# A hybrid diffusion step on one core: the products of the second four gates, spread over the four units of a long convolution

## Chip, core and metric

The kernel runs on one core of a Trainium2 chip. The metric is the device time of one execution in microseconds (us). The core's engines work from queues of their own: TensorE (PE in the rows, its weight loads PEld), VectorE (DVE), ScalarE (ACT), GpSimd (POOL) and SyncE (SP, which issues the transfers). Each engine takes its instructions strictly in order, and waits where an operand is not ready.

## What is computed

One inference step of a backbone with four layers: a Hyena long convolution, latent attention, RWKV-7, and a Hyena long convolution again. Only the two Hyena layers, the first and the last, are touched. Cut to what matters, the reference computes in each of them, for 1024 latent tokens and 128 context tokens and a width of 1024:

```python
u = h @ w_in                                   # 1024 x 4096
u3, z = u[..., :3 * HY_WIDTH], u[..., 3 * HY_WIDTH:]
prev, nxt = _neighbours(u3)
u3 = prev * conv_w[0] + u3 * conv_w[1] + nxt * conv_w[2] + conv_b
x0, x1, v = jnp.split(u3, 3, axis=-1)
v = v * x1
vf = jnp.fft.rfft(v, n=2 * L, axis=1)
kf = jnp.fft.rfft(filt, axis=0)
y = jnp.fft.irfft(vf * kf[None], n=2 * L, axis=1)[:, :L] + v * skip
return (y * x0 * jax.nn.silu(z)) @ w_out
```

## The kernel before

**Numbers.** All products are float32 in three passes: each operand is split in a high part (ACT, line 267) and a low part (POOL or DVE, line 268), and `mm3` (lines 260 to 264) issues high times high, high times low, low times high. One three-pass product of a 128x128 weight block with 384 tokens is three rows `ps_mm<-hh,wh`, `<-hl,wh`, `<-hh,wl`. They are called *product rows* here.

**Dense products.** `dense_jobs` (line 477) goes through a list of jobs. A job is one block of 128 columns of `w_in`; it has three *steps*, one for each group of 384 tokens, and a step is 24 product rows. After a step the job's own `evac` takes the result out of PSUM. A job for `v`, `x1` or `x0` ends with the convolution of three neighbours: two DVE rows on line 1006. Then `v * x1` is one DVE row on line 1023. A *gate* is the pair of jobs for `x0` and `z` of one block (`jobs_gate`, line 1031): eight gates in a layer. From the fifth on they are "late" (line 1034): ACT applies SiLU to each step's result (line 1047), DVE multiplies it by `x0` at once (line 1040, four pieces), and SP writes it out (line 1049).

**The long convolution** runs in four *units* of 256 channels (`conv_long`, line 1078), one after the other. A unit has three *stages*. *Forward*: transposes of `v` on PE (line 1073), ACT copies them to `xt` (line 1075), and some 42 DVE rows (lines 642 to 711) make eight residues. *Residue*: nine residues go through PE (`ps_fw`), DVE (line 1108), POOL (lines 1110 and 1111), ACT and POOL splits, and PE again (`ps_iv`): 210 PE rows in a unit. *Inverse*: some 47 DVE rows (lines 713 to 800) make `yc`, which SP writes to DRAM (line 1148). `xt` and `yc` use one buffer, so the next unit's copies to `xt` wait until that write has landed. What follows the fourth unit is `boundary` (line 497), the product with `w_out`; its first tile needs `yc` of all four units.

**What sets the order.** `GATES` (line 220) says how many gates go beside each part of the layer: the first number is for the making of the filters ahead of the units, the other four are for the units. `hyena` (lines 1150 to 1158) makes one list of jobs from it, in which the `v` and `x1` jobs of a unit stand beside the unit before, and `steps[q + 1]` is how many steps unit `q` is given. `weave` (line 165) hands out the turns of the unit, of the dense steps and of the modulation parts (`mod_part`, lines 290 to 330; eight DVE rows on line 302 and eight POOL rows on line 305 for a part) in proportion. This is only the order in which the program is written. A scheduler, which follows a timeline of its own, then sets the order on each engine, and moves rows far from where they were written.

Of the kernel before, what the change touches and what calls it, by code (L numbers as in the profile page):

```python
# [216 lines left out]
NM = 52  # L217
NE = 12
MZ = 12
GATES = (4, 0, 0, 0, 4)  # L220


class Prog:
# [745 lines left out]
    def hyena(self, i, j, lead, rest):  # L969
# [46 lines left out]
        def jobs_vx(q):  # L1016
            def dst(b):
                if b == 0:
                    vxs[q] = pool.tile([P, 2, W], F32, tag="vx", name="vx")
                return vxs[q][:, b]  # L1020

            def times(b):
                return lambda x1: v.tensor_tensor(vxs[q][:, b], vxs[q][:, b], x1, ALU.mult)

            r = []
            for b in range(2):
                r.append(conv3(16 + 2 * q + b, lambda b=b: dst(b), lambda d: None))
                r.append(conv3(8 + 2 * q + b, row, times(b)))
            return r

        def jobs_gate(b):

            s = {}
            late = b >= GATES[0]

# [115 lines left out]
        b = 0  # L1151
        for q, n in enumerate(GATES):
            new = jobs_vx(q) if q < NU else []
# [1185 lines left out]
```

## Time and profile before

| | us |
|---|---|
| median of three runs | 4577.58 |
| lowest and highest of the three | 4571.88, 4580.07 |
| the profiled execution's own time | 4590.18 |
| its span, first to last instruction | 4588.4 |
| the four units of the first layer in it, first copy to `xt` to last write of `yc` | 457.3 |
| the four units of the last layer in it | 415.4 |

The page and the queries of the trace are of the profiled execution. TensorE's records are pipelined, so the distance between two starts is what a row costs, not its duration. A stretch's granted clock is 1.00 at 2.4 GHz and 0.5 at 1.2 GHz; values between are means over the stretch.

### The profile page before, as it was taken

How to read it: one execution, taken by the hardware profiler on the slowest of the kernel's cores; microseconds unless marked ns; L12 is line 12 of the kernel's file. 1: busy time of each engine (PE TensorE's matmuls, PEld its weight loads, DVE VectorE, ACT ScalarE, POOL GpSimd, SP SyncE). 2: the span in 40 equal slices, each digit the busy share in tenths (PEclk: the TensorE clock that was granted, in tenths of full speed). 3: DMA queues.
4: the chain of work that ended last, by engine and by line, in shares of the span. 5: the costliest groups of instructions: out<-in, count | busy, mean ns of one | idle time of the engine just before them, and what ended most of it. 6: DMA issues, size and time to landing. Idle time of an engine off the chain costs nothing. (4 is left out here: it accounts for less than half of the span.)

```text
span 4588.4 us, 83899 instructions
## 1 busy us (share of the span) xinstructions
PE 4061.0 (89%) x30888; PEld 3510.6 (77%) x30888; DVE 3504.3 (76%) x6147; ACT 2392.5 (52%) x5468; POOL 2360.3 (51%) x1902
## 2 busy tenths in 40 slices
PE   7988988889999999879979786999999889988988
PEld 4888888678777776658867575878888678878986
DVE  7777888655998999687587997677767668967877
ACT  5554433455666666453455553666666456543331
POOL 3655766253677877455555564333333233466550
PEclk8999999999999999989988797999999899999999
DMA  5755555643000000326635464222322424665455
GB/s 169 239 181 176 164 156 157 191 149 99 19 22 21 18 28 30 121 91 203 188 108 198 145 222 136 59 79 84 83 75 68 142 93 120 214 205 153 141 155 179
DMA packets 490982, 583.04 MB, mean 127 GB/s; under 512 B 59818, under 2 KB 378332, under 8 KB 489932
## 3 DMA queue, kind: packets, MB, share of 16 engines
q1 hardware_dynamic: 489068, 576.70, 40.7%
q8 instruction: 244, 4.00, 0.4%
q14 instruction: 166, 1.36, 0.1%
q10 hardware_dynamic: 1504, 0.98, 0.1%
HBM read 413.74 MB, written 161.37 MB: 125 GB/s over the span
## 5 line engine op out<-in xcount | busy, mean ns | idle before, releaser
L262 PE MATMUL ps_mm<-hh,wh 128*128 128x384 f32 x1728 | 597.0, 347 | 47.4 <-ACT hh L267 24.0
L263 PE MATMUL ps_mm<-hl,wh 128*128 128x384 f32 x1728 | 595.6, 345 | 2.8 <-DVE hl L268 1.8
L264 PE MATMUL ps_mm<-hh,wl 128*128 128x384 f32 x1728 | 594.5, 344 | 2.7 <-POOL wl L268 2.7
L1499 POOL TENSOR_TENSOR sm<-sm,pf 128x512 f32<-128x512 f32 x288 | 443.4, 1540 | 121.8 <-ACT pf L1492 48.8
L268 POOL TENSOR_TENSOR wl<-wraw,wh 128x512 fp32r<-128x512 f32 x212 | 331.5, 1581 | 187.4 <-ACT wh L267 175.3
L262 PEld LDWEIGHTS ps_mm<-hh,wh 128*128 128x128 f32 x1728 | 335.9, 195 | 55.5 <-ACT hh L267 25.1
L1497 DVE TENSOR_TENSOR wl<-pf,wh 128x512 fp32r<-128x512 f32 x288 | 352.8, 1235 | 6.6 <-ACT wh L1493 5.8
L263 PEld LDWEIGHTS ps_mm<-hl,wh 128*128 128x128 f32 x1728 | 336.2, 195 | 7.5 <-DVE hl L268 4.4
L264 PEld LDWEIGHTS ps_mm<-hh,wl 128*128 128x128 f32 x1728 | 336.0, 194 | 6.4 <-POOL wl L268 3.8
L305 POOL TENSOR_TENSOR macc<-macc,mprod 128x512 f32<-128x512 f32 x140 | 211.8, 1513 | 178.0 <-ACT mprod L304 155.4
L263 PE MATMUL ps_mm<-mx,wh 128*128 128x384 f32 x680 | 253.6, 373 | 37.9 <-DVE mx L1669 36.9
L262 PE MATMUL ps_mm<-mx,wh 128*128 128x384 f32 x680 | 255.9, 378 | 19.9 <-ACT mx L1668 6.1
L262 PE MATMUL ps_mm<-woh,hh 128*128 128x512 f32 x576 | 233.8, 407 | 37.0 <-ACT hh L267 34.6
L2144 POOL TENSOR_TENSOR tot<-SV,wcs 64x128 f32<-64x128 f32 x288 | 115.6, 405 | 267.9 <-DVE SV L2172 245.2
L264 PE MATMUL ps_mm<-mx,wl 128*128 128x384 f32 x680 | 247.0, 364 | 3.1 <-POOL wl L268 3.1
L1492 ACT ACTIVATE pf<-ps_st 128x512 f32<-128x512 f32 x288 | 172.3, 598 | 144.9 <-POOL sm L1499 53.3
L264 PE MATMUL ps_mm<-woh,hl 128*128 128x512 f32 x576 | 234.1, 406 | 3.7 <-DVE hl L268 3.7
L302 DVE SCALAR_TENSOR_TENSOR macc<-modw,cond,macc 128x512 f32<-128x512 f32 x140 | 156.5, 1118 | 103.3 <-DMA modw<-mod_w 102.4
L1437 DVE TENSOR_REDUCE mx<-ps_pj 128x1 f32<-128x512 f32 (+2 forms) x400 | 220.4, 575 | 17.2 <-PE ps_pj L1436 16.4
L263 PE MATMUL ps_mm<-wol,hh 128*128 128x512 f32 x576 | 231.8, 402 | 0.0
L304 ACT ACTIVATE mprod<-modw,cond 128x512 f32<-128x512 f32 x140 | 101.3, 723 | 205.5 <-POOL macc L305 108.6
L1493 ACT ACTIVATE wh<-ps_st 128x512 fp32r<-128x512 f32 x336 | 194.3, 578 | 0.0
(560 smaller groups left out, 13149.2 us busy)
## 6 DMA issues: line engine op xcount, KB each, us to landing
cst<-cst SPq DMA_DIRECT2D x175, 384.0 KB
modw<-mod_w SPq DMA_DIRECT2D x160, 256.0 KB
wraw<-hy_w_in SPq DMA_DIRECT2D x128, 256.0 KB
kd<-kt SPq DMA_DIRECT2D x72, 384.0 KB
kt<-kd SPq DMA_DIRECT2D x72, 384.0 KB
cst<-cst SPq DMA_DIRECT2D x41, 512.0 KB
ctd<-ct SPq DMA_DIRECT2D x24, 768.0 KB
bkd<-bk SPq DMA_DIRECT2D x24, 768.0 KB
```

The costliest lines, as they stand in the source:

```text
L262: mm(ps, lh, rh, start=start, stop=False)
L263: mm(ps, lh, rl, start=False, stop=False)
L264: mm(ps, ll, rh, start=False, stop=stop)
L268: (lo_eng or self.nc.gpsimd).tensor_tensor(lo, src, hi, ALU.subtract)
L302: nc.vector.scalar_tensor_tensor(acc[0], w, s, acc[0], op0=ALU.mult, op1=ALU.add)
L305: nc.gpsimd.tensor_tensor(acc[1], acc[1], wp, ALU.add)
L1437: nc.vector.tensor_reduce(mx[:, t, j:j + 1], ps, AX.X, ALU.max)
L1492: nc.scalar.activation(pf, s, AF.Exp, scale=scale)
L1493: nc.scalar.activation(ph, s, AF.Exp, scale=scale)
L1497: nc.vector.tensor_tensor(pl, pf, ph, ALU.subtract)
L1499: nc.gpsimd.tensor_tensor(sm, sm, pf, ALU.add)
L2144: g_.tensor_tensor(tot[h], SV[e][h, jsl], wc[h].unsqueeze(2).broadcast_to([64, 2, 64]), M)
```

## The change

One number table changes; nothing that is computed does.

```diff
-GATES = (4, 0, 0, 0, 4)
+GATES = (4, 1, 1, 1, 1)
```

`steps` goes from (36, 12, 12, 12, 24) to (36, 18, 18, 18, 6): gates 4, 5, 6 and 7 are written beside units 0, 1, 2 and 3 in place of all beside unit 3. Which gates are "late" stays, since `GATES[0]` does. No instruction is added or removed on PE, DVE, ACT or POOL, and the same transfers are issued. What the scheduler makes of it on three places follows.

DVE at the end of the first unit's inverse, first layer. Lines 796, 799 and 754 are the inverse, 1040 a piece of a gate, 302 a modulation step, 651 the first row of the next unit. Before:

```order
L792 SCALAR_TENSOR_TENSOR st<-st 128x256
L302 SCALAR_TENSOR_TENSOR macc_4531<-modw,cond,macc_4531 128x512
L1023 TENSOR_TENSOR vx<-vx,xx 128x1153
L992 MEMSET up 128x1 x3
L796 TENSOR_TENSOR st<-st 128x256
L799 TENSOR_TENSOR st<-st 128x256
L993 MEMSET xx 128x1
L754 SCALAR_TENSOR_TENSOR yc<-st,yc 128x2x128 x2
```

And now:

```order
L1040 TENSOR_TENSOR xx<-xx 128x384
L302 SCALAR_TENSOR_TENSOR macc_4676<-modw,cond,macc_4676 128x512
L796 TENSOR_TENSOR st<-st 128x256
L799 TENSOR_TENSOR st<-st 128x256
L302 SCALAR_TENSOR_TENSOR macc_4676<-modw,cond,macc_4676 128x512
L754 SCALAR_TENSOR_TENSOR yc<-st,yc 128x2x128 x2
L796 TENSOR_TENSOR st<-st 128x256
L799 TENSOR_TENSOR st<-st 128x256
L993 MEMSET vx 128x1 x2
L302 SCALAR_TENSOR_TENSOR macc_4676<-modw,cond,macc_4676 128x512
L1040 TENSOR_TENSOR xx<-xx 128x256
L1040 TENSOR_TENSOR xx<-xx 128x128
```

Right behind this piece stand the last two rows on line 754: the pieces of gate 4 have moved in front of the end of the first unit's inverse.

DVE at the end of the last unit's inverse, last layer. Line 1006 is the convolution for gate 7, 1191 and 268 `hl` are the boundary's. Before:

```order
L785 SCALAR_TENSOR_TENSOR st<-st 128x256
L787 TENSOR_TENSOR st<-su 128x256
L1006 SCALAR_TENSOR_TENSOR xx<-up,cw,xx 128x1153
L788 TENSOR_TENSOR st<-su 128x256
L1191 TENSOR_TENSOR wh<-wh,wl 128x768
L1006 SCALAR_TENSOR_TENSOR xx<-up,cw,xx 128x1153
L791 SCALAR_TENSOR_TENSOR st<-st 128x256
L792 SCALAR_TENSOR_TENSOR st<-st 128x256
L268 TENSOR_TENSOR hl<-wh,hh 128x6x128
L1040 TENSOR_TENSOR xx<-xx 128x384
L796 TENSOR_TENSOR st<-st 128x256
```

And now:

```order
L785 SCALAR_TENSOR_TENSOR st<-st 128x256
L787 TENSOR_TENSOR st<-su 128x256
L788 TENSOR_TENSOR st<-su 128x256
L791 SCALAR_TENSOR_TENSOR st<-st 128x256
L792 SCALAR_TENSOR_TENSOR st<-st 128x256
L796 TENSOR_TENSOR st<-st 128x256
L799 TENSOR_TENSOR st<-st 128x256
L754 SCALAR_TENSOR_TENSOR yc<-st,yc 128x2x128 x2
```

The gate's and the boundary's rows have left the last inverse.

PE at the last inverse product of the last unit, last layer (`ps_iv`); `ps_mm<-woh,hh` is the boundary's first row. Before:

```order
L262 MATMUL ps_iv<-cst,zh 128x256
L263 MATMUL ps_iv<-cst,zh 128x256
L264 MATMUL ps_iv<-cst,zl 128x256
L263 MATMUL ps_mm<-hl,wh 128x384
L264 MATMUL ps_mm<-hh,wl 128x384
```

And now:

```order
L262 MATMUL ps_iv<-cst,zh 128x256
L263 MATMUL ps_iv<-cst,zh 128x256
L264 MATMUL ps_iv<-cst,zl 128x256
L262 MATMUL ps_mm<-woh,hh 128x512
L263 MATMUL ps_mm<-wol,hh 128x512
```

Before, 143 product rows stood between the last inverse product and the boundary there (116 in the first layer); now none do, in either layer.

How many product rows stand on PE between the first `ps_fw` row of residue 1 and the unit's last `ps_iv` row, counted in the two orders:

| unit | first layer, before | now | last layer, before | now |
|---|---|---|---|---|
| 0 | 120 | 192 | 116 | 141 |
| 1 | 160 | 172 | 126 | 144 |
| 2 | 106 | 144 | 146 | 192 |
| 3 | 141 | 32 | 124 | 60 |

## Rows read from the trace of the kernel before

**Rows 1.** Page, part 1: busy us, share and instructions of each engine.

```profile
PE 4061.0 (89%) x30888; PEld 3510.6 (77%) x30888; DVE 3504.3 (76%) x6147; ACT 2392.5 (52%) x5468; POOL 2360.3 (51%) x1902
```

**Rows 2.** Windows, units of either layer: stretch, length; PE, PEld, DVE, ACT, POOL busy; clock; DMA.

```profile
354.80:812.10 457.30, 399.53 (x2431) 386.44 (x2429) 373.93 (x618) 180.91 (x355) 293.68 (x221) 0.94 0.53 162
...
4053.00:4468.40 415.40, 374.33 (x2310) 362.64 (x2308) 317.90 (x565) 156.51 (x317) 247.66 (x191) 0.95 0.51 156
```

**Rows 3.** Windows, first layer: residue, inverse stage of units 0 to 3; forward of 3.

```profile
372.80:427.50 54.70, 49.86 (x330) 47.34 (x330) 36.90 (x55) 21.65 (x43) 41.46 (x36) 0.97 0.64 203
427.50:469.00 41.50, 29.09 (x165) 28.70 (x164) 38.30 (x68) 13.44 (x26) 16.22 (x14) 0.84 0.37 116
...
490.80:553.40 62.60, 56.37 (x360) 54.40 (x361) 48.07 (x56) 26.25 (x51) 60.07 (x45) 0.95 0.64 202
553.40:597.00 43.60, 39.03 (x224) 38.39 (x221) 40.91 (x70) 17.05 (x33) 19.88 (x14) 0.96 0.40 121
...
617.30:663.90 46.60, 44.45 (x319) 43.56 (x320) 32.59 (x42) 17.92 (x35) 44.50 (x37) 1.00 0.75 233
663.90:705.00 41.10, 33.12 (x183) 32.33 (x181) 37.95 (x65) 12.87 (x25) 17.62 (x13) 0.91 0.43 128
705.00:722.20 17.20, 15.14 (x76) 14.82 (x76) 15.15 (x37) 6.40 (x13) 8.28 (x4) 0.81 0.32 90
722.20:777.90 55.70, 50.12 (x336) 48.80 (x337) 37.42 (x47) 21.28 (x40) 44.46 (x39) 0.97 0.64 196
777.90:812.10 34.20, 28.17 (x150) 26.37 (x148) 33.59 (x66) 12.34 (x23) 14.81 (x8) 0.95 0.51 143
```

**Rows 4.** Windows, last layer: residue, inverse stage of units 0 to 3.

```profile
4071.00:4129.50 58.50, 50.56 (x320) 46.82 (x319) 40.23 (x59) 21.57 (x43) 42.32 (x37) 0.94 0.63 194
4129.50:4173.20 43.70, 31.84 (x181) 31.16 (x179) 38.88 (x65) 14.85 (x30) 18.84 (x15) 0.84 0.37 107
...
4191.10:4238.70 47.60, 47.55 (x318) 47.21 (x319) 28.21 (x42) 19.98 (x39) 40.95 (x37) 0.94 0.72 221
4238.70:4271.90 33.20, 32.55 (x194) 32.23 (x193) 30.86 (x62) 11.24 (x27) 10.58 (x9) 1.00 0.34 103
...
4290.40:4341.40 51.00, 49.52 (x335) 48.29 (x336) 34.32 (x49) 20.99 (x42) 42.27 (x36) 0.97 0.68 210
4341.40:4368.30 26.90, 26.90 (x159) 26.90 (x158) 24.88 (x53) 7.64 (x16) 8.67 (x7) 1.00 0.41 128
...
4383.60:4435.40 51.80, 48.23 (x314) 47.62 (x315) 30.15 (x40) 16.54 (x33) 39.11 (x35) 0.93 0.58 182
4435.40:4468.40 33.00, 29.40 (x161) 27.63 (x159) 29.27 (x55) 11.62 (x23) 14.38 (x6) 1.00 0.42 123
```

**Rows 5.** Timeline of PE, two runs of rows: start, duration, row, idle before.

```profile
446.67 0.33 PE L262 MATMUL ps_mm<-hh,wh 128*128 128x384 f32 x1
...
448.58 0.34 PE L264 MATMUL ps_mm<-hh,wl 128*128 128x384 f32 x1
...
4434.09 0.28 PE L262 MATMUL ps_iv<-cst,zh 128*128 128x256 f32 x1
...
4435.05 0.28 PE L264 MATMUL ps_iv<-cst,zl 128*128 128x256 f32 x1
```

**Rows 6.** Groups of DVE by line: count, busy us, mean ns, idle before.

```profile
L1023 DVE TENSOR_TENSOR vx<-vx,xx 128x1153 f32<-128x1153 f32 x16 | 24.4, 1526 | 0.1
...
L302 DVE SCALAR_TENSOR_TENSOR macc<-modw,cond,macc 128x512 f32<-128x512 f32 x140 | 156.5, 1118 | 103.3 <-DMA modw<-mod_w 102.4
```

**Rows 7.** Groups of DVE in the last inverse of the last layer.

```profile
L1006 DVE SCALAR_TENSOR_TENSOR xx<-up,cw,xx 128x1153 f32<-128x1153 f32 x2 | 3.9, 1936 | 0.0
...
L1040 DVE TENSOR_TENSOR xx<-xx 128x384 f32<-128x384 f32 (+1 forms) x3 | 1.5, 507 | 0.0
...
L1191 DVE TENSOR_TENSOR wh<-wh,wl 128x768 f32<-128x768 f32 x1 | 1.0, 959 | 3.1 <-PE ps_mm L264 3.1
```

**Rows 8.** Timeline of PE: the wait ahead of the second unit's transposes, first layer.

```profile
461.33 1.97 PE L1073 MATMUL ps_tp<-ident,vx 128*128 128x128 f32 x8 [12.41 <-DVE up L992]
```

## The prediction

> **What bounds the kernel now.** I read part 1 of the page first. PE is busy for 89% of the span [rows 1], the most of all engines, but that share is a mean over stages with different limits. So I then read the windows over the two places that the change touches. The four units take 457.3 us in the first layer and 415.4 us in the last, 872.7 of 4588.4 us [rows 2]; all else keeps its instructions and, but for small shifts, its order. Last I read the same windows by stage [rows 3, 4], and what ends the waits there.
>
> The reader is to see three different limits. In a *residue* stage PE and POOL are both near full: POOL 44.50 of 46.60 us in unit 2 of the first layer, 60.07 of 62.60 in unit 1, PE 49.52 of 51.00 in unit 2 of the last [rows 3, 4]. In an *inverse* stage of the first layer DVE is full: 38.30 of 41.50, 40.91 of 43.60, 37.95 of 41.10, 33.59 of 34.20 [rows 3]. In the last layer PE has hardly a gap from unit 1's residue stage to unit 2's end: 47.55 of 47.60 and 26.90 of 26.90 [rows 4]. The units follow each other through one buffer, so a unit is a chain of its three stages, and dense products only fill PE beside it. Products that sit between a unit's own rows in PE's queue lengthen it as soon as PE has no gap left; gate rows in DVE's queue lengthen an inverse.
>
> PE waits long in one kind of place: 12.41 us ahead of the second unit's transposes in the first layer [rows 8]. The products that the change brings into unit 0 fill it. That alone gains nothing, since DVE is busy all through that stage; it puts PE ahead by as much.
>
> **The change part by part.** No engine gains or loses rows, so all is a matter of where they stand. Prices: a product row costs 0.173 us (446.67 to 448.58 is eleven of them), a row of `ps_fw` or `ps_iv` 0.12 (4434.09 to 4435.05 is eight) [rows 5]. So a unit's 210 own rows are 25 us of PE, and a residue stage with n products needs n x 0.173 + 25 us of it. On DVE a convolution is two rows, 3.9 us together [rows 7], a row of `v * x1` is 1.53 us, a modulation row 1.12 [rows 6], a gate's piece 0.51, so 2.0 for four [rows 7].
>
> *Residue stages of units 0 to 2.* With the counts in the table of the two orders: first layer, unit 0 needs 58.2 us in place of 45.8 and took 54.70; some of its idle time is filled, so I put it at 60, +5.5. Unit 1 needs 54.8 and took 62.60 with POOL full: no change. Unit 2 needs 49.9 in place of 43.3 and took 46.60: 53, +6.5. Last layer: unit 0 needs 49.4 and took 58.50 on waits of other kinds, +1; unit 1 needs 49.9 in place of 46.8 and took 47.60, +3; unit 2 needs 58.2 in place of 50.3 and took 51.00, +8. Sum **+24**. From below it is 0, if waits that the rows show give way for all of it (PE idle 4.8, 6.2, 2.2, 7.9, 0.1 and 1.5 us in these six stages); from above 24 and those waits again, some +40. I take 24, near to the rows without a gap.
>
> *Forward and inverse stages of units 0 to 2.* Read from DVE's order. First layer: four pieces come into unit 0's inverse and one modulation row leaves it (+1); seven modulation rows leave unit 1's, the pieces and a `v * x1` row come (-4.5); unit 2's forward stage gets five modulation rows and loses a convolution (+2), its inverse gets a convolution, `v * x1` and one modulation row (+6.5). Last layer: pieces into unit 0's inverse (+2); a convolution into unit 1's forward stage (+4), one out of its inverse against the pieces (-2); a convolution and `v * x1` into unit 2's inverse (+5.5). Sum +14.5 if all of it lands. The six inverse stages hold 18 us in which DVE is idle (3.2, 2.7, 3.2, 4.8, 2.3, 2.0 [rows 3, 4]), so from below it is 0. I take **+7**, half, since either end has rows for it.
>
> *The last unit.* First layer: a convolution enters its forward stage and two pieces less run there (+3.5 on 17.20). Its residue stage loses 109 of 141 products: PE needs 30.5 us, and the cover is then POOL, 44.46 busy. I take 48 for 55.70: -8 (from -11 to 0). Its inverse was 34.20 with DVE full. Out of it go a convolution (3.9), the pieces (2.0) and the boundary's row 1191 and its split of the same shape (1.9 for both) [rows 7], together 7.8; with less work of POOL beside it I put it at 24, -10. Last layer: residue stage 51.80 to 44 (POOL 39.11), -8; inverse 33.00 to 21.5, since the same rows go and the wait of 3.1 us for a product [rows 7] with them: -11.5. Sum **-34**, from -45 (stages at POOL's and DVE's bare time) to -18 (residue stages unchanged, since transfers for nine residues come in the same row).
>
> *The end.* Before, 116 and 143 products covered PE during the last inverse; now nothing does. That costs nothing by itself: the boundary's first tile waits for `yc` in either case. SP issues the same transfers; gate writes now stand ahead of the write of `yc` in units 0 to 2, and wait there for pieces that DVE's order has in front of it anyway.
>
> Sum: +24 + 7 - 34 = -3 us against the profiled execution's 4590.18, so 4587. That execution was 12.6 us above the median of the runs, and I carry the difference over to it: 4577.58 - 3 = **4575 us**.
>
> *The clock.* The seventeen stages that have a row here ran at a granted clock of 0.93 or more but four: unit 0's inverse in either layer (0.84), in the first layer that with the wait of rows 8; one other inverse stage (0.91); and the last unit's forward stage in the first layer (0.81) [rows 3, 4]. The last unit's residue stages now hold 30 to 35 us of PE work in 44 to 48, a smaller share than any residue stage has in the rows. The Trainium skill (TensorE: Matmul & The Clock Gate, "What's actually happening") says that half rate is the default state and that activity releases it. By that rule part of these stages would run at half speed, and the sum would come out above the time before; by the rows as they stand it is -3. I make it a rival below.
>
> **Rivals.** *A: the early units hold their pace.* PE's wait of 12.41 us is filled and PE runs ahead by that, so the +24 and +7 shrink to some +5 while -34 stays: about -29, 4549 us. For it: 18 us of DVE and 23 us of PE idle in the stages concerned. Against it: unit 2 of the last layer, where PE has no gap to give.
>
> *B: slower, by the gate's pieces in DVE's queue.* In units 0 to 2 the inverse's last rows now stand behind the gate's pieces, so `yc` cannot end before the gate's last product but one. PE reaches that some 144 products and 18 transposes after the last `ps_iv`, 27 us, and ACT, DVE and the rest of the rows add 2. The inverse stages took 41.50, 43.60, 41.10, 43.70, 33.20 and 26.90 us, of which some 5 are the wait for the write [rows 3, 4]: room of 8 to 10 us in four of them, none in the last two. From the point where PE loses more than that room, every microsecond delays the next unit and all that follows. At 4 us for each of six units it is +24 on the sum: +21, 4599 us. For it: PE waits of 12 us exist. Against it: the change fills the one that is known.
>
> *C: slower, by the clock in the thinned last unit.* At 1.2 GHz a spacing doubles, so the residue stages would need 61 and 71 us of PE in place of 48 and 44, +40; half of each stage there gives +20: +17, 4595 us. Against it: the 55.70 us stage with waits inside stayed at 0.97 [rows 3].
>
> *D: the change does not do what it says.* The scheduler had already moved products ahead: the counts before are far from 12, 12, 12 and 24 steps. Then the time stays within the measurement; my forecast is near to it anyway.
>
> **How the numbers follow.** This kernel's measurement tells 0.2%, 9 us, from no change. My forecast with D: 0.47, own range -15 to +8, of which 0.13 is below -9 and 0.34 within. A: 0.26, from -14 to -45, all faster. B: 0.18, from +6 to +35. C: 0.09, from +9 to +30. Of B 0.01 lies within. So faster 0.39, same 0.35, slower 0.26. With a tenth left out at either end, the range runs from about -32 to +20: 4546 to 4598 us.
>
> **What would show it.** In the profile after, the windows by stage: the residue stages of unit 0 (first layer) at about 60 and unit 2 (last layer) at about 59 us, the last inverses at about 24 and 21.5, the last residue stages at about 48 and 44 with POOL near full. The wait of rows 8 should be gone. The fourth unit should start some 15 to 18 us later in either layer than before, counted from the first copy to `xt`. If it starts no later, A is right; if later by over 25 us, with DVE idle ahead of pieces of a gate (line 1040, released by ACT), B is. Half clock over more than a third of the last residue stages would be C. I would be wrong altogether if the time went into the attention or RWKV layers, whose rows shift a little in the order.

## The result, and the profile after

The changed kernel is slower: 4612.18 us (median of four, 4609.14 to 4621.68) against 4578.82, a ratio of 1.0077 with a 95% interval of 1.0056 to 1.0098. That is +33 us where -3 was forecast, and outside the range of 4546 to 4598. The profiled execution took 4621.68 us, its span 4619.9: 31.5 us more than before. Executions of one kernel lie up to some 30 us apart (before, in one row of runs: 4572.52 to 4601.36), and a trace is of one execution, so sums over two traces that differ by 10 or 20 us decide little; the medians do.

The page after, part 1, and then the windows over the four units of either layer (stretch, length; PE, PEld, DVE, ACT, POOL busy; clock; DMA share, GB/s), answer to [rows 1, 2]:

```profile
PE 4068.9 (88%) x30888; PEld 3513.1 (76%) x30888; DVE 3492.9 (76%) x6147; ACT 2387.2 (52%) x5468; POOL 2351.0 (51%) x1902
```

```profile
354.05:831.20 477.15, 403.58 (x2431) 387.62 (x2429) 370.86 (x615) 179.64 (x355) 284.24 (x221) 0.92 0.51 157
4073.85:4502.55 428.70, 377.91 (x2312) 363.75 (x2310) 320.95 (x566) 154.60 (x318) 248.67 (x191) 0.95 0.50 153
```

The units grew from 457.3 to 477.15 and from 415.4 to 428.70 us, +33.1 together, which is all of it. Rows and busy times of the engines hardly changed, so what changed is how much of the work lies beside other work. The stages of the first layer, as in [rows 3] (units 0 to 2: residue, inverse; unit 2's forward stage ahead of its own; all three of unit 3):

```profile
372.00:430.85 58.85, 58.63 (x398) 58.02 (x398) 33.41 (x57) 24.64 (x50) 43.28 (x37) 1.00 0.65 197
430.85:479.25 48.40, 44.28 (x244) 41.67 (x243) 42.34 (x73) 15.26 (x31) 21.09 (x14) 0.96 0.38 118
...
502.30:570.30 68.00, 55.87 (x363) 54.96 (x362) 48.49 (x62) 27.26 (x54) 51.51 (x43) 0.92 0.61 193
570.30:599.60 29.30, 29.30 (x182) 29.20 (x182) 26.25 (x62) 8.28 (x18) 6.47 (x5) 1.00 0.28 88
599.60:625.95 26.35, 21.18 (x113) 20.45 (x111) 24.40 (x35) 12.95 (x25) 15.57 (x10) 0.94 0.40 120
625.95:687.55 61.60, 52.23 (x350) 51.22 (x350) 38.58 (x58) 23.53 (x49) 46.83 (x39) 0.94 0.59 190
687.55:735.10 47.55, 42.90 (x248) 42.48 (x248) 42.42 (x69) 15.12 (x32) 21.25 (x16) 0.94 0.41 120
735.10:748.45 13.35, 12.44 (x70) 11.48 (x68) 11.27 (x23) 6.86 (x15) 2.98 (x2) 0.96 0.49 151
748.45:804.70 56.25, 38.97 (x232) 36.41 (x232) 41.74 (x58) 17.12 (x30) 39.66 (x36) 0.82 0.58 188
804.70:831.20 26.50, 9.07 (x34) 7.08 (x34) 25.47 (x55) 6.58 (x11) 11.32 (x6) 0.68 0.41 119
```

The same of the last layer, as in [rows 4] (residue, inverse of each unit; unit 2's residue stage from the row on that waited for its operand `sl`, as the 4290.40 of [rows 4] is):

```profile
4091.75:4148.90 57.15, 51.83 (x346) 50.66 (x346) 36.37 (x55) 23.07 (x47) 43.20 (x37) 0.97 0.62 194
4148.90:4197.35 48.45, 42.72 (x244) 40.09 (x242) 42.35 (x73) 15.24 (x31) 21.07 (x14) 1.00 0.39 117
...
4215.85:4274.95 59.10, 52.23 (x349) 51.31 (x349) 35.68 (x54) 22.92 (x48) 42.16 (x37) 0.94 0.64 191
4274.95:4306.20 31.25, 31.25 (x188) 31.08 (x188) 28.02 (x62) 8.97 (x22) 11.10 (x7) 1.00 0.31 100
...
4319.95:4382.35 62.40, 58.81 (x397) 58.12 (x398) 36.67 (x52) 24.62 (x51) 50.10 (x41) 1.00 0.63 197
4382.35:4414.10 31.75, 31.75 (x193) 31.58 (x192) 27.92 (x57) 8.95 (x22) 11.14 (x7) 1.00 0.33 103
...
4429.80:4480.10 50.30, 39.38 (x242) 37.34 (x242) 34.95 (x44) 14.28 (x25) 34.15 (x31) 0.87 0.57 179
4480.10:4502.55 22.45, 7.43 (x18) 5.21 (x18) 21.71 (x48) 5.13 (x9) 5.77 (x4) 0.65 0.32 94
```

Unit by unit, from first copy to first copy: +11, -8, +28, -11 us in the first layer; +3, +10, +11, -12 in the last. Three things are to be seen. Unit 0's inverse grew by 6.9 and 4.8 us, and DVE's busy time in it by 4.0 and 3.5, with the gate's four pieces in it. Unit 1's inverse in the first layer fell by 14.3: it lost the modulation rows, and unit 2 got them. And the last unit's residue stage, which lost three quarters and half of its dense products, stayed as it was: 56.25 for 55.70, 50.30 for 51.80.

### The profile page after: what moved, and what is told of

It is laid out like the page before. It is cut to its first block, busy times and chain, and to the rows that moved or that the text cites. A ratio compares the mean times of both kernels' runs of the same rounds, so it can differ in the third digit from the quotient of the medians.

```text
span 4619.9 us, 83929 instructions
## 1 busy us (share of the span) xinstructions
PE 4068.9 (88%) x30888; PEld 3513.1 (76%) x30888; DVE 3492.9 (76%) x6147; ACT 2387.2 (52%) x5468; POOL 2351.0 (51%) x1902
```

## Which gate costs, and where

Three runs write one gate alone beside an early unit (`GATES` as shown), and one leaves the change as it is but makes gates 4 to 6 in one go after their third step.

```diff
-GATES = (4, 1, 1, 1, 1)
+GATES = (4, 1, 0, 0, 3)   # move_u0; (4, 0, 1, 0, 3) move_u1; (4, 0, 0, 1, 3) move_u2
```

> Gates (4, 1, 0, 0, 3): only one gate is moved, from the last unit to unit 0, in either layer. In the profile after the change unit 0 is longer by 11.1 us in the first layer and 3.0 in the last, and the last unit shorter by 11.1 and 11.6 for three gates. Theory 'each gate costs where it is put': +14 for unit 0, a third of -23 for the last unit, so about +6 us, 4585. Theory 'product rows on PE' (a gate is 144 product rows, the same price in each unit: 55.6 us for three gates, 18.5 each): +11 us, 4590. Theory 'the unit that follows pays': units 1 and 2 change too although they get no gate, and the sum is not that of the profile.

> Gates (4, 0, 1, 0, 3): only one gate is moved, to unit 1. After the change unit 1 is shorter by 7.6 us in the first layer and longer by 10.2 in the last. Theory 'each gate costs where it is put': +2.6 and a third of -23, about -5 us, 4574. Theory 'product rows on PE': +11 us, 4590. Theory 'the unit that follows pays': unit 2 is longer, as it is after the change (+27.5 and +11.4), and the sum is about +10 or more.

> Gates (4, 0, 0, 1, 3): only one gate is moved, to unit 2. After the change unit 2 is longer by 27.5 us in the first layer and by 11.4 in the last. Theory 'each gate costs where it is put': +39 and a third of -23, about +31 us, 4610. Theory 'product rows on PE': +11 us, 4590. Theory 'the unit that follows pays': unit 2 stays near its length before, and the time within 10 us of 4579.

Measured against before: move_u0 1.0004 (0.9986 to 1.0021), move_u1 1.0051 (1.0036 to 1.0065), move_u2 1.0004 (0.9985 to 1.0022). To read them, one has to see where the scheduler put the gates. A gate has three SiLU rows on ACT (line 1047). How many of them start beside units 0 to 3 in each trace:

| kernel | first layer | last layer |
|---|---|---|
| before | 0, 0, 4, 8 | 0, 0, 3, 9 |
| after, nolow_spread, both_spread | 3, 3, 3, 3 | 3, 3, 3, 3 |
| move_u0 | 3, 0, 4, 5 | 3, 0, 3, 6 |
| move_u1 | 0, 3, 2, 7 | 0, 3, 0, 9 |
| move_u2 | 0, 0, 4, 8 | 0, 0, 3, 9 |
| one_last | 0, 0, 9, 3 | 0, 0, 9, 3 |
| one_spread | 3, 3, 6, 0 | 3, 3, 6, 0 |
| nolow_last | 0, 0, 4, 8 | 0, 0, 4, 8 |
| nodve_last | 0, 0, 3, 9 | 0, 0, 3, 8, and one behind |
| nodve_spread | 3, 2, 4, 3 | 3, 2, 3, 4 |
| both_last | 0, 0, 6, 6 | 0, 0, 6, 6 |

Written beside unit 3, gate 4 stood beside unit 2 already in the kernel before, in either layer. So the change takes two gates out of the last unit and not three, and move_u2 is in effect the kernel before: its time says nothing about a gate beside unit 2. move_u1 takes gate 4 from unit 2 to unit 1, and that costs 23 us (16 to 30); where they lie its trace can't tell, since it is of the fastest of the eleven executions (4593.97 us, median 4606.86), with units that take 873.8 us together, near the 872.7 of before. move_u0 takes one gate from the last unit to unit 0 for +2 us (-6 to +10): not the +11 of one price for each gate, while +6 is within. The third expectation, that the unit which follows pays, holds in move_u1 for the first layer (unit 2 at 128.2 us for 108.0) and not for the last (96.1 for 96.5). One thing stands out in move_u0's stages: with one gate gone, its last unit is as short as after the change (93.6 and 91.1 us against 96.1 and 88.5). So the second gate taken out of the last unit brings nothing that these traces show.

```diff
-            late = b >= GATES[0]
+            late = b == 7
```

> The changed kernel, with the gates of units 0 to 2 (4, 5 and 6) made as the first four are: ACT copies each step, and SiLU, the multiplication by x0 and one write follow after the third step. Theory 'gate pieces and gate writes in the queues of DVE and SP hold the unit': their number falls from 4 to 2 rows and from 3 to 1 writes for a gate and none waits for a step in the middle, so half or more of the +33 us goes, 4595 or less. Theories 'product rows on PE' and 'rows of DVE lengthened while POOL works': neither count changes, so the time stays within 8 us of 4612.

whole_spread: 1.0049 (1.0030 to 1.0069), some 13 us of the 35 that the ratio of the change stands for. That is between the two expectations, and its interval overlaps that of the change; by itself it settles nothing.

## Which engine charges for it

Each pair leaves out one engine's rows of gates 4, 5 and 6 in both orders of work. The rows on the other engines stay, but the scheduler makes the order anew for each kernel: the table above tells how near each stays to the one that it is made from. If an engine sets the price, the difference between the two kernels of its pair goes.

PE: one pass in place of three, 288 product rows fewer in either layer.

```diff
-                self.mm3(o, wh[:, k], wl[:, k], self.hh[g][:, k], self.hl[g][:, k], k == 0, k == KC - 1)
+                if len(jobs[n]) > 3 and jobs[n][3]:       # gates 4, 5, 6
+                    self.nc.tensor.matmul(o, wh[:, k], self.hh[g][:, k], start=k == 0, stop=k == KC - 1)
+                else:
+                    self.mm3(o, wh[:, k], wl[:, k], self.hh[g][:, k], self.hl[g][:, k], k == 0, k == KC - 1)
```

> The kernel before (gates 4 to 7 beside the last unit), with the products of gates 4, 5 and 6 made in one pass in place of three: 288 of PE's product rows are left out in either layer, 50 us each at 0.173 us. The control for the next kernel; it says what those rows cost beside the last unit. Theory 'product rows on PE': up to 100 us less in all, since the last unit and the end behind it hold most of them. Theories of DVE, POOL or queues: less than half of that.

> The changed kernel with the same 288 rows of gates 4, 5 and 6 left out in either layer. Against the control: theory 'product rows on PE': the change's +33 us falls to a third, +12 us or less. Theory 'rows of DVE lengthened while POOL works' and theory 'queues' (all rows of DVE, POOL and SP are still there): it stays at +25 to +40 us.

one_last 1.0003 (0.9991 to 1.0016), one_spread 1.0053 (1.0033 to 1.0073). A hundred microseconds of PE's rows were left out and the kernel before did not become faster. The difference is still 0.50%, 23 us (12 to 34), between the 12 or less of one theory and the 25 to 40 of the others. The pair is not a clean one: in one_last all three gates stand beside unit 2, in one_spread two do and none beside unit 3, and unit 0's inverse takes 57.9 us there in place of 48.4. Fewer products and another order are mixed in both, so that dense products have no price of their own is not shown.

POOL: the low parts of these gates' weights are not made (24 rows).

```diff
-        self.load_split(wh, wl, src)
+        if not low:                                       # gates 4, 5, 6
+            for ks in (slice(0, 4), slice(4, KC)):
+                raw = self.wp.tile([P, 4, P], F32, tag="wraw", name="wraw")
+                nc.sync.dma_start(raw, src.rearrange("(k p) n -> p k n", p=P)[:, ks])
+                nc.scalar.copy(wh[:, ks], raw)
+            return wh, wh
```

> The kernel before, with the low part of the weights of gates 4, 5 and 6 not made (the high part stands in for it in the products, so PE's rows are all there): 12 POOL rows of 1.55 us are left out in either layer. The control for the next kernel. Theory 'rows of DVE lengthened while POOL works': a POOL row costs DVE about 1.1 us where DVE is full, so up to 26 us less. Theory 'product rows on PE': no change beyond 8 us.

> The changed kernel with the same 24 POOL rows left out. Against its control: theory 'rows of DVE lengthened while POOL works': the rows now stand beside stages that DVE fills, so the change's +33 us falls by some 15 to 25 us. Theory 'product rows on PE' and theory 'queues': it stays within 8 us of +33.

nolow_last 0.9963 (0.9947 to 0.9979), nolow_spread 1.0037 (1.0024 to 1.0049). Both nearly keep the order of their kernels and became faster, by 17 and 18 us for 37 us of POOL rows, but the difference stayed at 0.74%, 34 us. POOL's rows cost time wherever they stand; they don't make the change's price.

DVE: the two convolution rows and four pieces of these gates are not made.

```diff
-                for k, off in ((0, 0), (2, 2)):
+                for k, off in () if 4 <= col < 7 else ((0, 0), (2, 2)):
...
             def times(lo, hi):
+                if 4 <= b < 7:
+                    return
```

> The kernel before, with DVE's rows of gates 4, 5 and 6 left out (the two convolution rows for x0 and the four pieces of the multiplication, 5.9 us for a gate, 17.7 for a layer); products, splits, SiLU and writes stay. The control for the next kernel. Theory 'DVE is full in forward and inverse stages, but beside the last unit it has room': at most 10 us less in all.

> The changed kernel with the same rows of DVE left out, 35 us in both layers. Theory 'DVE's rows of the gates set the price': units 0 to 2 get most of those 35 us back, and against its control the change costs +10 us or less in place of +33. Theory 'the order and the queues set it' (PE, POOL and SP still have all their rows): it stays at +25 or more.

nodve_last 1.0005 (0.9992 to 1.0018), nodve_spread 1.0004 (0.9991 to 1.0017). This is the answer, as far as the runs give one. As they stood before, those 35 us of rows were free: without them the kernel before is no faster. Where the change puts them they cost 33 us (22 to 45), their whole time: without them the change costs nothing. It is not simply the last unit against the early ones, since some 20 of the 35 us (8 of 12 convolution rows, 9 of 24 pieces) stood beside unit 2 before. Why they were free there is not shown. The windows over the units of nodve_spread, and below them those of its control nodve_last:

```profile
350.67:803.99 453.32, 396.11 (x2428) 383.67 (x2426) 340.80 (x596) 178.74 (x354) 292.26 (x221) 0.93 0.54 166
4053.74:4469.10 415.36, 374.44 (x2310) 362.66 (x2308) 295.88 (x548) 155.00 (x317) 249.66 (x191) 0.95 0.51 158
```

```profile
354.76:804.60 449.84, 396.39 (x2421) 383.84 (x2420) 353.95 (x600) 179.85 (x355) 280.56 (x221) 0.94 0.54 165
4047.66:4450.70 403.04, 367.01 (x2287) 356.92 (x2287) 296.08 (x546) 156.53 (x316) 245.08 (x191) 0.96 0.53 160
```

868.7 us in place of 905.9 after the change. The control's 852.9 are of its fastest execution (4570.50 us, median 4587.15; nodve_spread 4588.55, median 4587.02), so the 16 us between these two traces decide nothing. Against the trace of after, the gain lies in the inverse stages: the six of units 0 to 2 take 193.6 us in place of 236.7, and unit 0's are at 37.0 and 37.2 (48.4 and 48.5 with the rows). The residue stages did not shrink. Unit 2 of the first layer is still at 134.0 us and unit 1 at 111.3: unit 2 keeps the modulation rows that unit 1 lost.

Then each kind of row alone (the first or the second half of the diff above):

> The changed kernel with the convolution rows of x0 of gates 4, 5 and 6 left out (two rows, 3.9 us a gate, 23.6 us in both layers); the pieces stay. Leaving out both kinds took the change from +33 to +3 us. Theory 'time of DVE's rows': two thirds of that, 4612 to about 4592. Theory 'a piece waits for its product in DVE's queue': little of it, 4605 or more.

> The changed kernel with the pieces of the multiplication of gates 4, 5 and 6 left out (four rows, 2.0 us a gate, 12 us in both layers); the convolutions stay. Theory 'time of DVE's rows': one third, 4612 to about 4600. Theory 'a piece waits for its product in DVE's queue': nearly all, 4590 or less.

noconv_spread 1.0039 (1.0023 to 1.0055), nopiece_spread 1.0034 (1.0022 to 1.0046): 17 and 20 us less than the change, each known to some 12, which add up to it. That agrees with the rows' own time (23.6 and 12 us); a wait of the pieces, which asked for little from the convolutions and nearly all from the pieces, does not fit. What hangs on a row (a write that waits for a piece, a row behind it in DVE's queue) is left out with it, and the runs don't part that from its time. That a piece waits long for its product is not it: the two longest such waits in an inverse of units 0 to 2 after the change, in DVE's timeline of units 1 and 2 of the last layer, are

```profile
4302.94 2.00 DVE L1040 TENSOR_TENSOR xx<-xx 128x256 f32<-128x256 f32 x2 [0.78 <-ACT xx L1047]
...
4410.28 2.00 DVE L1040 TENSOR_TENSOR xx<-xx 128x256 f32<-128x256 f32 x2 [1.17 <-ACT xx L1047]
```

## Why DVE is full there: its rows wait for POOL

A forward row of 128x256 takes 0.41 us in some rows and 1.50 in others of the same form. The timelines of DVE and then of POOL over some eight microseconds of unit 2's forward stage after the change, first layer (start, duration, row, idle before):

```profile
605.14 1.50 DVE L656 SCALAR_TENSOR_TENSOR st<-st 128x256 f32<-128x256 f32 x1
606.56 0.75 DVE L666 TENSOR_TENSOR st<-xt 128x256 f32<-128x256 f32 x2
607.23 1.53 DVE L657 SCALAR_TENSOR_TENSOR st<-st 128x256 f32<-128x256 f32 x1
608.69 0.74 DVE L302 SCALAR_TENSOR_TENSOR macc<-modw,cond,macc 128x512 f32<-128x512 f32 x1
609.35 0.41 DVE L658 SCALAR_TENSOR_TENSOR su<-st,su 128x256 f32<-128x256 f32 x1
609.68 1.51 DVE L660 SCALAR_TENSOR_TENSOR su<-st,su 128x256 f32<-128x256 f32 x1
611.12 1.49 DVE L666 TENSOR_TENSOR st<-xt 128x256 f32<-128x256 f32 x1
```

```profile
604.80 1.55 POOL L305 TENSOR_TENSOR macc<-macc,mprod 128x512 f32<-128x512 f32 x1 [0.87 <-ACT mprod L304]
607.20 1.29 POOL L305 TENSOR_TENSOR macc<-macc,mprod 128x512 f32<-128x512 f32 x1 [0.84 <-ACT mprod L304]
609.32 1.59 POOL L305 TENSOR_TENSOR macc<-macc,mprod 128x512 f32<-128x512 f32 x1 [0.84 <-ACT mprod L304]
610.87 2.89 POOL L268 TENSOR_TENSOR wl<-wraw,wh 128x512 fp32r<-128x512 f32 x2
```

Each long row starts while a POOL row runs, and ends just behind it (606.64 for 606.35, 611.19 for 610.91). In the trace of before, the eight units have 744 rows of DVE with 128x256 in and out: 142 took over 0.8 us, and every one of them started while a POOL row ran and ended 0.28 to 0.29 us after it. A POOL row beside it does not always lengthen a row: 108 short ones started beside one, too, and for 92 of these it was the POOL row that took long, over 2 us (its shortest with 128x512 is 1.26). The Trainium skill (SBUF — State Buffer, "Who interferes with whom") says that a DVE instruction with two SBUF inputs contends with a GpSimd instruction that reads SBUF, and that the one issued second blocks until the first has ended. The rows agree, in either direction. A busy time of DVE therefore holds waiting that the page does not show as idle. An estimate for unit 0's inverse after the change, first layer, with each form of DVE row priced at the time of its short ones: some 13 of the 42.34 us, beside 21.09 us of POOL rows.

If so, a row taken from POOL and given to DVE should make both shorter. In the Hyena layers the low part of the dense weights (128 rows) and the second modulation product (140 rows on POOL, and 140 on ACT) go to DVE:

```diff
-        dense = self.dense_jobs(jobs)
+        dense = self.dense_jobs(jobs, v)                  # lo_eng of load_split
...
-                wp = self.mp.tile([P, 512], F32, tag="mprod", name="mprod", bufs=1)
-                nc.scalar.activation(wp, w, AF.Copy, scale=sp)
-                nc.gpsimd.tensor_tensor(acc[1], acc[1], wp, ALU.add)
+                nc.vector.scalar_tensor_tensor(acc[1], w, sp, acc[1], op0=ALU.mult, op1=ALU.add)
```

> The kernel before, with two kinds of POOL rows given to DVE: the low part of the dense weights in the Hyena layers (128 rows of 1.55 us on POOL) and the second modulation product (140 rows of 1.55 us on POOL, and 140 on ACT; on DVE one row of line 302's form, 0.66 us where nothing lengthens it). Theory 'a DVE row waits while POOL works, so the two are one resource': DVE gets 170 us more rows and is still no later, since 415 us of POOL rows go: 20 to 80 us less in all. Theory 'DVE is the bound and POOL has room': 30 us or more are added.

> The changed kernel with the same rows moved from POOL to DVE. Against both_last: theory 'one resource': a gate costs an early unit less (its four POOL rows are gone, four shorter DVE rows come), so the change costs about +20 us in place of +33. Theory 'the order and the queues set it': +33 as before, within 10. Theory 'DVE alone': more than +33.

> The kernel before, with the low part of the dense weights of the Hyena layers made on DVE in place of POOL (128 rows), and the modulation left as it is. both_last, which moves the modulation's 140 rows too, was at 4506 us, 78 less than before. Theory 'each POOL row taken from beside a full DVE gives about as much': half of it, 4545 (4530 to 4560). Theory 'the modulation alone gives it, since its rows stand in the inverse stages and it frees ACT too': 4570 or more.

both_last, with `GATES` as before the change, took 4505.91 us: 0.9831 (0.9811 to 0.9851), 77 us less than before, and faster than both kernels. wl_last, the weights alone, 0.9919 (0.9898 to 0.9940), near half of it. The order differs a little, too: both_last has two gates beside unit 2, before had one. both_spread 0.9900 (0.9878 to 0.9922): the change still costs 0.69%, 32 us (18 to 45), with these POOL rows gone and those of the residues left. That is as 'the order and the queues' had it, and the 20 us of 'one resource' is not excluded. So the lengthened rows are real and dear, but nothing shows that they are what makes the gates dearer beside the early units. The page of both_last, part 1, and then its groups of modulation and weight rows on DVE (count, busy us, mean ns, idle before):

```profile
PE 4040.6 (90%) x30888; PEld 3495.5 (78%) x30888; DVE 3501.2 (78%) x6415; ACT 2303.7 (51%) x5326; POOL 1980.9 (44%) x1634
```

```profile
L302 DVE SCALAR_TENSOR_TENSOR macc<-modw,cond,macc 128x512 f32<-128x512 f32 x140 | 130.9, 935 | 59.1 <-DMA modw<-mod_w 58.4
L303 DVE SCALAR_TENSOR_TENSOR macc<-modw,cond,macc 128x512 f32<-128x512 f32 x140 | 122.3, 873 | 10.4 <-ACT macc L300 8.4 <-DMA modw<-mod_w 1.9
...
L268 DVE TENSOR_TENSOR wl<-wraw,wh 128x512 fp32r<-128x512 f32 x128 | 97.4, 782 | 36.7 <-ACT wh L267 36.3
```

DVE has 268 more rows, 220 us of them, and is busy for 3501.2 us in place of 3504.3 [rows 1]: about as much has gone from the length of its other rows.

## Why the last unit's residue stage did not shrink

PE's longest wait in that stage after the change, first layer (who waited for whom, us in total, times, longest), is for constants. SP's timeline, below it, shows their issue behind a write of gate 7:

```profile
PE ps_fw L262 <- DMA cst<-cst: 12.3, 4, 4.1
```

```profile
741.53 0.55 SPq L1134 DMA_DIRECT2D ycd<-yp  x1
755.21 0.33 SPq L1049 DMA_DIRECT2D gd<-xx  x1
755.64 0.53 SPq L634 DMA_DIRECT2D cst<-cst  x1
```

Three runs took away one suspect each: the writes from SP's queue; the load of `kt`, a third of a residue's transfers, and SP's wait for it; and, with the gates as before, all of POOL's rows in the units.

```diff
-                    nc.sync.dma_start(gd[b, :, gs], s["z"][:, gs])
+                    nc.scalar.dma_start(gd[b, :, gs], s["z"][:, gs])          # act_spread
...
-                kt = pool.tile([P, 3 * UNIT], F32, tag="kt", name="kt", bufs=2)
-                nc.sync.dma_start(kt, self.kd[q, r])
+                if r == 8:                                                    # onekt_spread
+                    U["kt"] = pool.tile([P, 3 * UNIT], F32, tag="kt", name="kt", bufs=2)
+                    nc.sync.dma_start(U["kt"], self.kd[q, r])
+                kt = U["kt"]
...
-            self.split(zh, zl, z)
+            self.split(zh, zl, z, v)                                          # all_last, on top of both_last
-                nc.gpsimd.tensor_tensor(z[:, 0], z[:, 0], m[:, 0, 1], ALU.subtract)
+                v.tensor_tensor(z[:, 0], z[:, 0], m[:, 0, 1], ALU.subtract)
...
```

> The changed kernel with the writes of gates 4 to 7 issued by ACT in place of SP; nothing else differs. In the last unit of the first layer SP stood before a write of gate 7 from 742.1 to 755.2 us with the residues' transfers behind it. Theory 'gate writes in SP's queue keep the last unit long': its residue stages fall from 57.8 and 53.7 us to 50 or less, and the whole by 8 to 15 us to about 4600. Theory 'the residue stage has a floor of its own near 50 us': 4608 to 4614.

> The changed kernel with the filter's spectrum kt loaded once for a unit, for its first residue, in place of nine times (64 loads of 384 KB are left out in both layers, a third of a residue's transfers, and with them SP's wait on line 1104 for the DVE rows that free kt); the other residues use the first one's. Theory 'the transfers and SP's order set the floor of the residue stage': the last unit's residue stages fall from 56.3 and 50.3 us to 45 or less, the early units' by some us too, and the whole to 4590 or less. Theory 'the floor is the chain of a residue through ACT, PE, DVE and POOL': they stay within 3 us, and the whole at 4604 or more.

> The kernel before with every POOL row of the four units given to DVE: those of both_last (4506 us), and also the low parts of a residue's two splits and its sum and difference (lines 1110 and 1111). Theory 'DVE and POOL are one resource and POOL's rows set the floor of a residue stage': residue stages fall from 50 to 60 us to 45 or less, and the whole to 4480 or less. Rival 'DVE becomes the bound of the residue stage, since a row there now stands behind the dense products' rows': 4506 or more.

act_spread 1.0075 (1.0055 to 1.0095) and onekt_spread 1.0084 (1.0065 to 1.0103) are the change itself; all_last 0.9845 (0.9823 to 0.9868), 4517 us, is no faster than both_last, as its rival had it. The last unit's residue stages, here counted from the very first `ps_fw` row of residue 1, which puts the stages of after at 57.80 and 53.70: the windows of act_spread, then of onekt_spread, both_spread, all_last and one_spread, first layer and last.

```profile
747.30:799.50 52.20, 36.84 (x225) 34.20 (x223) 31.89 (x46) 15.73 (x27) 43.55 (x37) 0.84 0.62 199
4421.00:4473.60 52.60, 37.83 (x253) 35.59 (x252) 37.57 (x51) 15.83 (x31) 36.71 (x32) 0.90 0.60 186
```

```profile
743.70:798.90 55.20, 42.59 (x241) 39.84 (x240) 44.24 (x59) 18.29 (x31) 41.30 (x37) 0.78 0.49 149
4418.60:4472.80 54.20, 41.41 (x253) 39.18 (x252) 36.71 (x51) 15.97 (x31) 37.13 (x32) 0.89 0.44 136
```

```profile
708.00:758.30 50.30, 35.40 (x208) 32.09 (x208) 39.21 (x58) 13.62 (x24) 39.57 (x32) 0.77 0.61 190
4332.90:4383.60 50.70, 38.32 (x251) 35.67 (x249) 35.81 (x46) 14.30 (x26) 36.21 (x32) 0.90 0.65 194
```

```profile
689.60:743.00 53.40, 36.54 (x204) 34.47 (x202) 40.51 (x81) 12.89 (x22) 0.00 (x0) 0.74 0.56 175
4313.50:4356.20 42.70, 37.12 (x253) 35.43 (x251) 33.56 (x70) 15.54 (x29) 0.00 (x0) 0.96 0.63 187
```

```profile
750.70:806.55 55.85, 35.31 (x208) 31.95 (x208) 30.76 (x52) 16.20 (x27) 45.24 (x37) 0.76 0.53 168
4410.10:4458.50 48.40, 31.21 (x192) 28.36 (x192) 25.06 (x44) 12.89 (x22) 37.36 (x32) 0.83 0.53 160
```

With products or without, with a third of the bytes gone, with POOL idle, it stays at 48 to 57 us, but once (42.70, in one layer of all_last). In act_spread the forward stage ahead grew from 11.8 to 17.9 us, so the first layer's 52.20 is a shift and no gain. The lower clock need not cost: both_spread at 0.77 has the same 50 us in the first layer as both_last at 0.87 (its window 695.55:746.15). So no one of PE's products, POOL, and the bytes of `kt` sets the length alone.

For the gate's writes it is not settled, since act_spread puts them in the queue of an engine that a residue needs. What PE waited for in its first layer's stage:

```profile
PE ps_iv L262 <- ACT zh L267: 6.7, 4, 3.1
PE ps_fw L262 <- DMA cst<-cst: 5.4, 4, 1.8
```

The wait for constants fell from 12.3 to 5.4 us, and that for ACT's part of a residue rose from 1.1 to 6.7. all_last gave POOL's rows to DVE, and no run took DVE's own out of this stage. What sets it (the latency of a residue through five engines with two buffers, or the constants' buffers) stays open.

## Why the prediction was wrong, by its own steps

*Residue stages of units 0 to 2, +24.* This held in the main. From the very first `ps_fw` row of residue 1, by which the products were counted, the six stages grew by 4.1, 6.3, 10.7 us in the first layer and -1.8, 4.4, 6.3 in the last, +30. (The start is not sharp: the first rows stand up to seven us ahead of the others, and by windows that begin with the others, like [rows 3, 4], it is +46, at the expense of the forward stages.) The price of a product row is of use only where PE has no gap: unit 2 of the last layer, 192 products for 146, grew by 6.3 for the 8 that were told, unit 0 of the first layer by 4.1 for 72 products. One reading was wrong: the text set 50.3 us of PE work against a stage of 51.00, but the 146 products lie in 56.8.

*Forward and inverse stages, +7.* This is the step that failed: that about half of the DVE rows which come to the early units would go into time in which DVE was idle. Measured from the same first rows, the forward stages grew by 19 us and the inverse stages by 7, +26. The 18 us of DVE's idle time in the six inverse stages were no room: after the change they are 27, 3.0 to 6.1 in each. Some 11 of the 18 lay behind the stage's last `yc` row, where the next unit waits for the write (4.4 to 5.5 us from that row to the first copy, before as after), and a gate's row in front of that row lengthens the stage all the same. And the pair without DVE's rows of gates 4 to 6 gives their price: nothing as they stood before, 33 us where the change puts them, which is all of their 35 within the interval. The count of +14.5, "all of it", is of rows that change their unit, less modulation rows that move on to the next; it would have been nearer and still short, and what lies between it and the measured +26 is not taken apart.

*The last unit, -34.* Mis-sized: measured -22.7 (-11.0 and -11.7). The inverse stages came near to what was told: 26.50 and 22.45 for 24 and 21.5. The residue stages did not: 56.25 and 50.30 for 48 and 44. The text took POOL as the cover; POOL is busy for 39.66 of the 56.25, and in the run without POOL's rows the two stages took 53.40 and 42.70, where after has 57.80 and 53.70 by the same count. Why they stay long is open.

So +24 + 7 - 34 became +30 + 26 - 23: all three terms were off to the same side, by 6, 19 and 11 us. DVE's rows are the only ones whose absence made the change cost nothing (nodve_spread is at the time of before); that the products' +30 and the last unit's -23 then about cancel is an account that fits, and no run shows it by itself.

*What would show it.* The wait of [rows 8] is gone, and unit 0's residue stage came at 58.85 for 60. The fourth unit started 30.9 and 24.9 us later, not 15 to 18: past the 25 that the text gave as a sign of rival B in the first layer, and just short of it in the last. B's other sign, DVE idle ahead of the pieces, is hardly there (0.78 and 1.17 us). B had the right engine and the right side, and +33 lies within its range; but its price of 4 us a unit was for a wait of the pieces; the rows' own time is 5.9.

*Rival C* was in part on: the last unit's residue stages ran at 0.82 and 0.87, so by an estimate from these means a third and a quarter of them at half clock, as the rule of the Trainium skill would have it that the prediction cites (TensorE: Matmul & The Clock Gate, "What's actually happening"). The first is just at the sign that was given, over a third; no time follows from it that the runs can tell.

*Rivals A and D* were wrong in the time. PE did fill its wait of 12.41 us, and unit 0 still grew, as the first part of the prediction had it for a stage that DVE fills. D's reason was in part right: the scheduler had one gate beside unit 2 already, so the change takes two gates out of the last unit.

## What to carry to other kernels

Price moved work by the engine that is full in the stage that receives it, and at its full time: idle time in that stage is no room until one has seen where in the stage it lies. Here rows of DVE that were free in one order cost all of themselves in another. To find the engine, leave out one engine's rows of the moved work in the kernel before and in the one after, and look which pair's difference goes; and where a scheduler makes the order, count in the traces where the moved work came to stand, before trusting a pair or an edit: one run here changed the text and hardly the order, and one pair changed both. Where DVE and POOL both work in a stage, read DVE's rows one by one: a form with two durations is a wait that the page counts as busy, and giving two-input rows from POOL to DVE can be worth more than the schedule (here 1.7%).

## What had not been expected of the hardware

A DVE row of 128x256 with two inputs takes 0.41 us where nothing lengthens it; behind a POOL row that runs it can take up to 1.55, and each of the 142 long ones ended 0.28 to 0.29 us after that POOL row. Handing 268 rows from POOL (and 140 from ACT) to DVE left DVE's busy time as it was (3501.2 for 3504.3 us) and took 77 us off the kernel. And 576 product rows fewer on PE, 100 us, changed the time by 0.03%, in a kernel whose gates the scheduler then placed otherwise.
